# The last stage of a mixture-of-experts layer: one gate matrix per 64 tokens, the residual accumulated in PSUM, normalisation in two vector operations

## The chip, the core and the metric

The kernel runs on one core of a Trainium2 chip. The metric is the device time of one execution in microseconds (us). A core has five engines that run side by side and wait for each other through semaphores: TensorE (PE in the profile), VectorE (DVE), ScalarE (ACT), GpSimd (POOL) and SyncE (SP, which issues most transfers). PE writes its results to PSUM, in banks of 512 float32 numbers per partition; everything else lies in SBUF (128 partitions) or in HBM.

## The reference, cut to what matters

One encoder layer over 1024 tokens of 1024 numbers: a mixer, a layer norm that gives `x1`, and a mixture of experts in which each token takes two experts out of 32. The change touches only how the two experts' rows of a token are brought together and normalised:

```
gate  = pg_sel * softmax(top two expert logits)        # two gates a token
f     = gate[:,0]*expert_row_0 + gate[:,1]*expert_row_1
x     = layer_norm(ALPHA*x1 + g2*f) * ln2_gain + ln2_bias   # the output
layer_norm(z) = (z - mean(z)) * rsqrt(var(z) + 1e-5)   # over the 1024 numbers of a token
```

## The kernel before

Some 950 us go to the mixer, the rest to `experts()`. There the tokens are gathered by expert into blocks of up to 128, 64 or 32 rows; a block goes through gate and up projections (`head`, lines 1689 and 1697), a transposition (`turn`) and the down projection (`down`, lines 1717 and 1728). For blocks of 64 and 32 rows the matrix multiplications use 64 or 32 columns of the array each and write to their own part of the PSUM partitions. The rows, already multiplied by `g2`, are scattered to `ys_d` in HBM by POOL, so that row `2*token + j` holds the j-th expert's row of a token. Three weight buffers of each kind are used in turn, and once the experts are through, their space takes the data of the last stage.

The last stage begins in `finish` (line 1562) on SP: it loads the gain and bias (`late`), `x1` in two transfers (`x1a`, `x1b`, lines 1570 to 1573), waits for the last scattered rows, and loads `ys_d` in eight transfers of 1 MB, one for each tile of 128 tokens (line 1577). Before the change partition p of a tile holds both rows of token p, 8 KB in one piece.

`tail_plan` (line 1800) writes the work of the last stage on PE, ACT and DVE as three lists. Each engine runs its list in the written order and waits, ahead of an entry, for the entries named with it. For each of the eight tiles:

- `dg0`, `dg1`: diagonal 128x128 matrices with a tile's gates, one for each j, made once on ACT and DVE.
- `product` (PE): for each half of 512 numbers, `dg0` times the first rows plus `dg1` times the second, accumulated in a PSUM bank. In tiles 2 and 5 (`inside`) a third multiplication adds `ALPHA*x1`.
- `sums`: in tiles 2 and 5 ACT copies the bank to SBUF and sums it up on the way; in the other six DVE adds `ALPHA*x1` and sums up (`scalar_tensor_tensor`, line 1835).
- `mean` (DVE), `deviation` (ACT: `sq` sums up the squares, `sd` takes the root), `rstd` (DVE: reciprocal and one product), `normal` (ACT: `xn`, scale and shift in one), `affine` (DVE: times gain, plus bias).
- SP writes the tile out (line 1621) once `add` is done.

The products take three pairs of PSUM banks in turn (`pf`, line 1816), so the product of tile t waits for the sums of tile t-3. In float32 PE runs each multiplication of the lists as two instructions; the profile counts those.

Of the kernel before, what the change touches and what calls it, by code (L numbers as in the profile page):

```python
# [123 lines left out]
class Builder:  # L124
# [1336 lines left out]
    def experts(self):  # L1461
# [9 lines left out]

        gain, bias = self.late[:, 0], self.late[:, 1]
# [15 lines left out]
        names += [f"l{i}" for i in range(8)] + ["x1a", "x1b", "tail_pe", "tail_act", "tail_dve"]  # L1488
# [60 lines left out]
        tail = self.tail_plan(sem, yall, x1a, of, ls, gain, bias, [(pgu[0], pgu[1]), tuple(pT), tuple(py)], junk)  # L1549
        with nc.Block() as blk:  # L1550
            @blk.sync
            def _(e):
# [64 lines left out]
                e.dma_start(g2, self.rows_d[3]).then_inc(sem("g2"), 16)  # L1617
                step(0, None)
# [162 lines left out]
            def _(e):  # L1781
# [12 lines left out]

                pipeline(e, lambda g, t: evac_T(e, g, t, 1), head, lambda g, t: [out(e, g, t, q) for q in range(2)], None)
# [4 lines left out]
    def tail_plan(self, sem, yall, x1a, of, ls, gain, bias, banks, junk):  # L1800
# [8 lines left out]
        dg, eps = self.late[:, 2:4].rearrange("p a (j n) -> p (a j) n", n=128), self.leps  # L1809
        gates = self.gtw.rearrange("p j t -> p (j t)")  # L1810
        ident, alpha = self.C["ident"], self.C["alpha"]
# [3 lines left out]
        inside = lambda tt: tt in (2, 5)  # L1815
        pf = lambda tt: banks[tt % 3]

        def product(tt):
            def f(e):
                n = 3 if inside(tt) else 2  # L1820
                for h in range(2):
                    for j in range(n):
                        i = e.matmul(pf(tt)[h], dg[:, tt + 8 * j] if j < 2 else alpha,  # L1823
                                     (yall[tt][:, j] if j < 2 else x1a[tt])[:, hs[h]], start=j == 0, stop=j == n - 1)
                return i
            free = [("sum1", tt - 3)] if tt > 2 else []
            op("pe", "mm", tt, [("dg0", tt), ("dg1", tt), (f"l{tt}", 16), ("x1" + "ab"[tt // 4], 16)] + free, f)

        def sums(tt):
            for h in range(2):  # L1830
                if inside(tt):
                    op("act", f"sum{h}", tt, [("mm", tt)], lambda e, h=h: e.activation(
                        of[tt][:, hs[h]], pf(tt)[h], AF.Copy, accum_out=col(tt, h)))
                else:
                    op("dve", f"sum{h}", tt, [("mm", tt), ("x1" + "ab"[tt // 4], 16)], lambda e, h=h: e.scalar_tensor_tensor(  # L1835
# [3 lines left out]
        def mean(tt):  # L1839
            op("dve", "mean", tt, [("sum1", tt)], lambda e: e.tensor_scalar(  # L1840
                col(tt, 12), col(tt, 0), col(tt, 1), -1.0 / D, op0=OP.add, op1=OP.mult))

        def rstd(tt):
# [3 lines left out]
        def affine(tt):  # L1847
            op("dve", "gain", tt, [("xn", tt), ("late", 32)], lambda e: e.tensor_mul(of[tt], of[tt], gain))  # L1848
            op("dve", "add", tt, [("gain", tt)], lambda e: e.tensor_add(of[tt], of[tt], bias))  # L1849
# [7 lines left out]
        def normal(tt):  # L1857
            op("act", "xn", tt, [("rs", tt)], lambda e: e.activation(of[tt], of[tt], AF.Identity, bias=col(tt, 16),
                                                                    scale=col(tt, 15)))


        for tt in range(8):
            op("act", "dg0", tt, [], lambda e, j=tt: e.activation(dg[:, j], ident, AF.Copy, scale=gates[:, j:j + 1]))
            op("dve", "dg1", tt, [], lambda e, j=tt + 8: e.tensor_scalar(dg[:, j], ident, gates[:, j:j + 1], None,
                                                                        op0=OP.mult))
# [100 lines left out]
```

## Time and profile before

| | |
|---|---|
| time before, median of 3 runs | 1594.07 us (1593.53 to 1601.02) |
| the profiled execution | 1595.89 us, of which span 1594.0 us |
| busy over the span | PE 87%, DVE 49%, ACT 36%, POOL 24% |
| mean granted clock of PE | 0.915 of full speed |
| the last stage | from the first load of `ys_d` at 1541.62 to the end of the span |

A busy share is an average over stages with different limits. The last stage is some 52 us of 1594, and what a change there is worth is read from its own stretch: which engine the chain of waits runs through, when the first tile can begin, and what comes after the last sum. Times with two decimals that stand alone (1547.12) are us from the start of the span.

### The profile page before, as it was taken

The numbers are of one execution on the slowest core, as the hardware profiler recorded it, in microseconds if no ns is written. First come the engines' busy times: TensorE is split into PE (matmuls) and PEld (weight loads), VectorE is DVE, ScalarE is ACT, GpSimd is POOL, SyncE is SP. The second block draws the span as 40 slices with busy tenths as digits, with TensorE's granted clock in tenths as the row PEclk, the third lists the DMA queues.
The fourth block names the chain that finished last, engine by engine and source line by source line (L and its number), as shares of the span: only waits on it lengthen the run. The fifth ranks groups of instructions, "written<-read, shape, count | busy, mean of one in ns | idle before, by whom it ended". The sixth has DMA issues, their size and how long they took to land. (4 is left out here: it accounts for less than half of the span.)

```text
span 1594.0 us, 25797 instructions
## 1 busy us (share of the span) xinstructions
PE 1383.6 (87%) x8638; PEld 1014.9 (64%) x8638; DVE 779.3 (49%) x2015; ACT 573.9 (36%) x1196; POOL 379.0 (24%) x442
## 2 busy tenths in 40 slices
PE   6999999978869899899999728999998898789866
PEld 5778777766656677676788725676764575566522
DVE  6776786845974666655668851111111111111127
ACT  5663332414566777676444320000000010000006
POOL 3331332350347115601323141100110011101000
PEclk8999999987869899989999758999999999899978
DMA  9868999866413217117383648878978877887674
GB/s 256 221 195 309 290 296 332 285 221 179 134 51 105 80 41 204 39 53 219 95 322 121 250 173 353 338 296 305 376 275 310 334 298 279 333 337 307 253 268 201
DMA packets 163401, 371.94 MB, mean 233 GB/s; under 512 B 22880, under 2 KB 99009, under 8 KB 154227
## 3 DMA queue, kind: packets, MB, share of 16 engines
q1 hardware_dynamic: 155555, 350.59, 62.0%
q0 software_dynamic: 7632, 18.51, 3.6%
q8 instruction: 133, 2.18, 0.6%
q14 instruction: 81, 0.66, 0.1%
HBM read 365.47 MB, written 65.44 MB: 270 GB/s over the span
## 5 line engine op out<-in xcount | busy, mean ns | idle before, releaser
L1689 PE MATMUL m_pgu<-w,m_xT 128*128 128x256 f32 x896 | 200.1, 385 | 7.0 <-issue 7.0
L1689 PEld LDWEIGHTS m_pgu<-w,m_xT 128*128 128x128 f32 x896 | 171.5, 193 | 31.9 <-issue 8.2
L1697 PE MATMUL m_pgu<-w,m_xT 128*32 128x256 f32 (+1 forms) x1312 | 119.1, 459 | 38.8 <-issue 38.8
L1638 POOL DMA_INDIRECT ys_s<-m_y,m_idx x37 | 35.0, 946 | 494.4 <-DVE m_y L1756 299.9
L196 PE MATMUL pg<-uh,w_h 128*128 128x512 f32 x320 | 127.1, 404 | 2.2 <-ACT uh L294 1.6
L197 PE MATMUL pg<-ul,w_h 128*128 128x512 f32 x320 | 128.8, 402 | 0.2 <-POOL ul L295 0.2
L198 PE MATMUL pg<-uh,w_l 128*128 128x512 f32 x320 | 127.4, 398 | 0.0
L1697 PEld LDWEIGHTS m_pgu<-w,m_xT 128*32 128x32 f32 (+1 forms) x1312 | 56.6, 127 | 91.4 <-issue 76.4
L1789 DVE TENSOR_TENSOR m_h<-m_sil,m_pgu 128x256 f32<-128x256 f32 x28 | 11.8, 421 | 192.6 <-ACT m_sil L1765 192.6
L1717 PE MATMUL m_py<-w,m_hT 128*128 128x512 f32 x224 | 99.6, 597 | 0.0
L1793 DVE TENSOR_TENSOR m_h<-m_sil,m_pgu 64x256 f32<-64x256 f32 (+1 forms) x23 | 10.8, 471 | 160.2 <-ACT m_sil L1768 156.4
L1765 ACT ACTIVATE m_sil<-m_pgu 128x256 f32<-128x256 f32 x28 | 10.7, 383 | 196.1 <-PE m_pgu L1689 196.1
L210 DVE SCALAR_TENSOR_TENSOR acc<-wm,sc_c,acc 128x256 f32<-128x256 f32 x112 | 62.0, 554 | 31.9 <-DMA wm<-in_w_mod_dram 22.1
L1773 ACT COPY m_hT<-m_ph 128x128 f32<-128x128 f32 (+2 forms) x37 | 14.8, 401 | 165.3 <-PE m_ph L1705 165.3
L1717 PEld LDWEIGHTS m_py<-w,m_hT 128*128 128x128 f32 x224 | 41.4, 190 | 47.3 <-issue 46.9
L196 PEld LDWEIGHTS pg<-uh,w_h 128*128 128x128 f32 x320 | 61.0, 192 | 15.8 <-ACT uh L294 1.8
L197 PEld LDWEIGHTS pg<-ul,w_h 128*128 128x128 f32 x320 | 61.5, 192 | 14.4 <-POOL ul L295 0.9
L198 PEld LDWEIGHTS pg<-uh,w_l 128*128 128x128 f32 x320 | 61.4, 192 | 13.6 <-issue 0.7
L945 DVE SCALAR_TENSOR_TENSOR sn<-s,fc,sf 64x64 f32<-64x64 f32 x168 | 47.6, 283 | 41.8 <-PE s L936 38.7
L756 PE MATMUL g<-zi,bk 64*128 64x128 f32 x384 | 54.2, 319 | 15.2 <-DMA bk<-bkd 9.5
L1768 ACT ACTIVATE m_sil<-m_pgu 64x256 f32<-64x256 f32 (+1 forms) x23 | 9.8, 427 | 153.9 <-PE m_pgu L1697 153.9
L756 PEld LDWEIGHTS g<-zi,bk 64*128 64x128 f32 x384 | 46.5, 217 | 27.8 <-issue 10.3
(521 smaller groups left out, 3090.6 us busy)
## 6 DMA issues: line engine op xcount, KB each, us to landing
w<-in_moe_w_gate_dram SPq DMA_DIRECT2D x37, 2048.0 KB, 8.7
w<-in_moe_w_up_dram SPq DMA_DIRECT2D x37, 2048.0 KB, 12.9
w<-in_moe_w_down_dram SPq DMA_DIRECT2D x37, 2048.0 KB, 15.5
wm<-in_w_mod_dram SPq DMA_DIRECT2D x128, 128.0 KB, 4.5
w<-in_w_in_dram SPq DMA_DIRECT2D x21, 512.0 KB, 6.6
hd<-h SPq DMA_DIRECT2D x18, 512.0 KB, 4.5
wm<-in_w_mod_dram SPq DMA_DIRECT2D x16, 512.0 KB, 6.6
w<-ys_s SPq DMA_DIRECT2D x8, 1024.0 KB, 13.0
```

What stands on the lines that cost most here:

```text
L196: mm(out, lh[0], rh[0], start=start, stop=False)
L197: mm(out, lh[0], rh[1], start=False, stop=False)
L198: mm(out, lh[1], rh[0], start=False, stop=stop)
L210: nc.vector.scalar_tensor_tensor(acc, wm, self.sc_c[:, k:k + 1], acc, op0=OP.mult, op1=OP.add)
L756: nc.tensor.matmul(pa[h][:, j], bk[hs, j], zr[hs, j], start=True, stop=True)
L945: nc.vector.scalar_tensor_tensor(sn[H[h], H[h]], p[H[h], 2, H[h]], fc[H[h]], sf[H[h], H[h]], op0=OP.mult, op1=OP.add)
L1638: e.indirect_dma_start(out=self.ys_d, out_offset=off(idx[0:t, NP + g:NP + g + 1]), in_=y[0:t, g % NY], in_offset=None, bounds_check=2 * S ...
L1689: i = mm(pgu[q][:, o:o + 256], xT[:, k], w[:, k, 256 * q:256 * q + 256], start=k == 0, stop=k == 7)
L1697: i = mm(pgu[0][o:o + t, 0:n], xT[:, k, 0:t], w[:, k, c:c + n], start=k == 0, stop=k == 7)
L1717: i = mm(py[nh], hT[:, 128 * f:128 * f + 128], wd[b][:, f, 512 * nh:512 * nh + 512], start=f == 0, stop=f == 3)
L1773: e.copy(hT[:, 0:n], ph[:, 0:n]).then_inc(sem("hs"), 1)
L1789: e.tensor_mul(h[:, c], sil[:, c], pgu[q][:, 256:512]).then_inc(sem("h"), 1)
```

## The change

1. **One matrix for 64 tokens.** SP loads `ys_d` by another pattern: partition p of tile t now holds rows 256t+p and 256t+128+p, two pieces of 4 KB. Partition p of half s belongs to token 64s + p//2 and to j = p%2, so one 128x64 matrix (a one at column p//2, times the gate of row p) adds both gated rows of 64 tokens in one multiplication. `pair` holds the ones, `rowg` the gates in that order; `rowg` is filled by four small transfers at the start of `experts()`. A product is now four multiplications of 64 columns a tile (two halves of tokens, two of the 512), each to 64 of the PSUM partitions, and each half of 512 has a list entry of its own (`mm0`, `mm1`).
2. **`x1` into PSUM.** In tiles 0 to 6 (`inside`) `residual` multiplies `x1` by `ALPHA` times the identity into the banks first, and the products accumulate on it; ACT does their sums. Only tile 7 is added on DVE. The residuals of tiles 0 and 1 stand at the head of PE's list.
3. **Normalisation.** `centre` (`xm`) takes (z - mean)*gain and `normal` takes that times 1/deviation plus bias, each one `scalar_tensor_tensor` over 128x1024 on DVE. `xn` on ACT, the two vector operations of `affine` and the product `rs` go.

The core of the diff (the new wiring of the names through `experts()` is left out):

```diff
-                        e.dma_start(yall[tt], self.ys_d[256 * tt:256 * tt + 256, :].rearrange("(t j) n -> t j n", j=2)
+                        e.dma_start(yall[tt], self.ys_d[256 * tt:256 * tt + 256, :].rearrange("(s p) n -> p s n", s=2)
...
+                for s in range(2):
+                    for j in range(2):
+                        e.dma_start(rowg[j:128:2, s, :], self.gtw[64 * s:64 * s + 64, j, :]).then_inc(sem("rowg"), 16)
...
+                e.tensor_add(pair, ident[:, 0:128:2], ident[:, 1:128:2]).then_inc(sem("pair"), 1)
...
-        inside = lambda tt: tt in (2, 5)
+        inside = lambda tt: tt < 7
...
+        def residual(tt):
+            def f(e):
+                for h in range(2):
+                    i = e.matmul(pf(tt)[h], alpha, x1a[tt][:, hs[h]], start=True, stop=False)
+                return i
+            op("pe", "x1", tt, [("x1" + "ab"[tt // 4], 16)] + [(f"sum{h}", tt - 3) for h in range(2) if tt > 2], f)
...
+            def half(e, h):
+                for s in range(2):
+                    i = e.matmul(pf(tt)[h][64 * s:64 * s + 64, :], dg[:, 2 * tt + s], yall[tt][:, s, hs[h]],
+                                 start=not inside(tt), stop=True)
...
-            op("dve", "rs", tt, [("rec", tt)], lambda e: e.tensor_mul(col(tt, 16), col(tt, 12), col(tt, 15)))
-            op("dve", "gain", tt, [("xn", tt), ("late", 32)], lambda e: e.tensor_mul(of[tt], of[tt], gain))
-            op("dve", "add", tt, [("gain", tt)], lambda e: e.tensor_add(of[tt], of[tt], bias))
-            op("act", "xn", tt, [("rs", tt)], lambda e: e.activation(of[tt], of[tt], AF.Identity, bias=col(tt, 16),
-                                                                    scale=col(tt, 15)))
+        def centre(tt):
+            op("dve", "xm", tt, [("mean", tt), ("mm1", tt), ("late", 32)], lambda e: e.scalar_tensor_tensor(
+                xm(tt), of[tt], col(tt, 12), gain, op0=OP.add, op1=OP.mult))
+            op("dve", "add", tt, [("rec", tt), ("xm", tt), ("sq", tt)], lambda e: e.scalar_tensor_tensor(
+                of[tt], xm(tt), col(tt, 15), bias, op0=OP.mult, op1=OP.add))
...
+        for tt in range(2):
+            residual(tt)
         for tt in range(8):
+            if tt > 1 and inside(tt):
+                residual(tt)
             product(tt)
-        for tt in range(10):
-            if 0 < tt < 9:
-                rstd(tt - 1)
+        for tt in range(9):
             if tt < 8:
                 if not inside(tt):
                     sums(tt)
                 mean(tt)
-            if tt > 1:
-                affine(tt - 2)
-        for tt in range(9):
-            if tt < 8 and inside(tt):
-                sums(tt)
+                centre(tt)
             if tt:
                 normal(tt - 1)
-            if tt < 8:
-                deviation(tt)
+        for tt in range(8):
+            if inside(tt):
+                sums(tt)
+            deviation(tt)
```

Up to the last stage the order of every engine is the same but for `rowg` on SP and `pair` on DVE. PE's list for the tiles 0 to 2, before; `m_pgu`, `m_pT` and `m_py` are the three pairs of banks, `w_7635` a tile's rows, `m_xg` the gate matrices, `cst` the identity times ALPHA, and a row's last column its output:

```order
-L1823 MATMUL m_pgu<-w_7635,m_xg 128x512 [waits DMAHW6_49,m_x1a,m_tail_dve,m_tail_act]
-L1823 MATMUL m_pgu<-w_7635,m_xg 128x512 x3
-L1823 MATMUL m_pT<-w_7635,m_xg 128x512 [waits DMAHW7_49,m_tail_dve,m_tail_act]
-L1823 MATMUL m_pT<-w_7635,m_xg 128x512 x3
-L1823 MATMUL m_py<-w_7635,m_xg 128x512 [waits PE_49,m_tail_dve,m_tail_act]
-L1823 MATMUL m_py<-w_7635,m_xg 128x512
-L1823 MATMUL m_py<-w,cst 128x512
-L1823 MATMUL m_py<-w_7635,m_xg 128x512 x2
-L1823 MATMUL m_py<-w,cst 128x512
```

The same place now:

```order
+L1828 MATMUL m_pgu<-w,cst 128x512 [waits m_x1a]
+L1828 MATMUL m_pgu<-w,cst 128x512
+L1828 MATMUL m_pT<-w,cst 128x512 x2
+L1835 MATMUL m_pgu<-w_7635,m_xg 64x512 [waits DMAHW6_49,m_tail_dve,m_tail_act]
+L1835 MATMUL m_pgu<-w_7635,m_xg 64x512 x3
+L1835 MATMUL m_pT<-w_7635,m_xg 64x512 [waits DMAHW7_49,m_tail_dve,m_tail_act]
+L1835 MATMUL m_pT<-w_7635,m_xg 64x512 x3
+L1828 MATMUL m_py<-w,cst 128x512 x2
+L1835 MATMUL m_py<-w_7635,m_xg 64x512 [waits PE_49,m_tail_dve,m_tail_act]
+L1835 MATMUL m_py<-w_7635,m_xg 64x512 x3
```

Four multiplications that wait for `x1` alone now stand ahead of the first that waits for `ys_d`, and a tile has two of 128 and four of 64 columns instead of four (tiles 2 and 5: six) of 128.

DVE's list for the last three tiles, before (`m_ls` holds the columns of sums, means and deviations, `w_8648` the tiles themselves):

```order
-L1835 SCALAR_TENSOR_TENSOR w_8648,m_ls<-w,m_pT 128x512 [waits m_tail_pe]
-L1835 SCALAR_TENSOR_TENSOR w_8648,m_ls<-w,m_pT 128x512
-L1840 TENSOR_SCALAR m_ls<-m_ls 128x1 [waits m_tail_dve]
-L1848 TENSOR_TENSOR w_8648<-w_8648,m_xg 128x1024
-L1849 TENSOR_TENSOR w_8648<-w_8648,m_xg 128x1024 [waits m_tail_dve]
-L1844 RECIPROCAL m_ls<-m_ls 128x1 [waits m_tail_act]
-L1845 TENSOR_TENSOR m_ls<-m_ls 128x1 [waits m_tail_dve]
-L1848 TENSOR_TENSOR w_8648<-w_8648,m_xg 128x1024
-L1849 TENSOR_TENSOR w_8648<-w_8648,m_xg 128x1024 [waits m_tail_dve]
-L1848 TENSOR_TENSOR w_8648<-w_8648,m_xg 128x1024 [waits m_tail_act]
-L1849 TENSOR_TENSOR w_8648<-w_8648,m_xg 128x1024 [waits m_tail_dve]
```

The same end now, from the mean of tile 6:

```order
+L1853 TENSOR_SCALAR m_ls<-m_ls 128x1 [waits m_tail_act]
+L1860 SCALAR_TENSOR_TENSOR w_8648<-w_8648,m_ls,m_xg 128x1024 [waits m_tail_pe,m_tail_dve]
+L1864 RECIPROCAL m_ls<-m_ls 128x1
+L1865 SCALAR_TENSOR_TENSOR w_8648<-w_8648,m_ls,m_xg 128x1024 [waits m_tail_dve]
+L1848 SCALAR_TENSOR_TENSOR w_8648,m_ls<-w,m_pT 128x512 [waits m_x1b,m_tail_pe]
+L1848 SCALAR_TENSOR_TENSOR w_8648,m_ls<-w,m_pT 128x512 [waits m_tail_pe]
+L1853 TENSOR_SCALAR m_ls<-m_ls 128x1 [waits m_tail_dve]
+L1860 SCALAR_TENSOR_TENSOR w_8648<-w_8648,m_ls,m_xg 128x1024 [waits m_tail_dve]
+L1864 RECIPROCAL m_ls<-m_ls 128x1 [waits m_tail_act]
+L1865 SCALAR_TENSOR_TENSOR w_8648<-w_8648,m_ls,m_xg 128x1024 [waits m_tail_dve]
+L1864 RECIPROCAL m_ls<-m_ls 128x1 [waits m_tail_act]
+L1865 SCALAR_TENSOR_TENSOR w_8648<-w_8648,m_ls,m_xg 128x1024 [waits m_tail_dve]
```

The mean of tiles 0 to 6 now waits for ACT, the last gain and bias lie one tile behind instead of two, and `sums` stand on DVE only for tile 7.

ACT's list for the tiles 1 and 2 now (a tile is two copies with a sum, the squares, the root):

```order
+L1845 ACTIVATE w_7635,m_ls<-m_pT 128x512 [waits m_tail_pe] x2
+L1869 ACTIVATE w,m_ls<-w_7635,m_ls 128x1024 [waits m_tail_dve]
+L1871 ACTIVATE m_ls<-m_ls,m_le 128x1 [waits m_tail_act]
+L1845 ACTIVATE w_7635,m_ls<-m_py 128x512 [waits m_tail_pe] x2
+L1869 ACTIVATE w,m_ls<-w_7635,m_ls 128x1024 [waits m_tail_dve]
+L1871 ACTIVATE m_ls<-m_ls,m_le 128x1 [waits m_tail_act]
```

Within a tile ACT now waits for DVE's mean between its sums and its squares, and nothing of another tile stands in between.

## Rows read from the trace of the kernel before

**Rows 1.** The page's first line.

```profile
span 1594.0 us, 25797 instructions
```

**Rows 2.** Chain of waits, 1540 to 1594: start, us, engine or transfer, line.

```profile
1541.62 5.25 DMA w<-ys_s
...
1547.12 5.97 PE m_pgu L1823 x8
1553.09 3.43 PE m_pT L1823 x8
...
1573.73 1.27 ACT w L1832 x4
```

**Rows 3.** Timeline, last 4 us: start, duration, engine, line, operation.

```profile
1589.77 1.23 DVE L1849 TENSOR_TENSOR w<-w,m_xg 128x1024 f32<-128x1024 f32 x1
1591.03 0.33 SPq L1621 DMA_DIRECT2D out_dram<-w  x1
```

**Rows 4.** Stretches: us, busy by engine (instructions), granted clock, DMA share, GB/s.

```profile
core 0: us, PE busy (x) PEld busy (x) DVE busy (x) ACT busy (x) POOL busy (x), PEclk, DMA share, GB/s
...
1526.00:1528.00 2.00, 1.32 (x25) 0.58 (x13) 1.28 (x3) 0.00 (x0) 0.00 (x0) 1.00 1.03 414
1535.00:1537.00 2.00, 0.72 (x4) 0.00 (x0) 1.25 (x2) 0.67 (x3) 0.00 (x0) 1.00 0.00 0
1549.00:1551.00 2.00, 2.00 (x4) 0.97 (x3) 0.00 (x0) 0.00 (x0) 0.00 (x0) 0.50 0.98 406
1560.00:1580.00 20.00, 20.00 (x48) 8.74 (x46) 16.11 (x36) 15.95 (x29) 0.00 (x0) 1.00 0.43 173
```

**Rows 5.** Chain of waits in two expert blocks, down projection, 64 and 128 rows.

```profile
1004.37 3.58 PE m_py L1728 x16
...
1499.64 7.06 PE m_py L1717 x16
```

**Rows 6.** Timeline, ACT and DVE in the last stage, 1555 to 1576.

```profile
1555.98 1.28 ACT L1854 ACT_TABLE_LOAD   x1
...
1566.48 0.68 DVE L1835 SCALAR_TENSOR_TENSOR w<-w,m_pgu 128x512 f32<-128x512 f32 x1
...
1567.20 0.21 DVE L1840 TENSOR_SCALAR m_ls<-m_ls 128x1 f32<-128x1 f32 x1
...
1567.45 1.15 ACT L1852 ACTIVATE w<-w,m_ls 128x1024 f32<-128x1024 f32 x1 [0.23 <-DVE m_ls L1840]
...
1568.73 0.29 ACT L1854 ACTIVATE m_ls<-m_ls,m_le 128x1 f32<-128x1 f32 x1
...
1575.03 0.21 DVE L1840 TENSOR_SCALAR m_ls<-m_ls 128x1 f32<-128x1 f32 x1 [0.82 <-ACT w L1832]
```

**Rows 7.** Timeline, DVE and POOL in the mixer, 152 to 157 and 278 to 284.

```profile
154.12 1.28 DVE L655 SCALAR_TENSOR_TENSOR o_k<-z,cw,o_k 128x1024 f32<-128x1024 f32 x1
155.32 0.42 DVE L432 SCALAR_TENSOR_TENSOR row<-pm,bm 128x256 f32<-128x256 f32 x1
...
279.00 1.47 POOL L722 TENSOR_TENSOR kd<-kd,kd 128x512 f32<-128x512 f32 x1
279.24 2.31 DVE L654 SCALAR_TENSOR_TENSOR o_k<-z,cw,o_k 128x1024 f32<-128x1024 f32 x1
```

**Rows 8.** Lines 1571 and 1577: issue (ns, first and last start), time to landing.

```profile
L1571 SPq DMA_DIRECT2D w<-x_s x2: 432/470/508, 1517.3 to 1517.7; - x2
DMA to landing us min/median/max: 10.7/13.2/15.7
...
L1577 SPq DMA_DIRECT2D w<-ys_s x8: 332/456/755, 1541.6 to 1545.3; - x8
DMA to landing us min/median/max: 5.3/13.0/19.7
```

**Rows 9.** Start of `experts()`: SP's first transfer, PE's first expert product.

```profile
L1617 SPq DMA_DIRECT2D m_g<-rows_s x1: 326/326/326, 949.6 to 949.6; - x1
...
956.09 6.18 PE L1697 MATMUL m_pgu<-w,m_xT 128*32 128x256 f32 x64 [0.61 <-issue]
```

**Rows 10.** Timeline, the gate matrices on DVE before the last stage.

```profile
1538.88 1.66 DVE L1864 TENSOR_SCALAR m_xg<-cst,m_gt 128x128 f32<-128x128 f32 x8 [1.75 <-issue]
```

More of the change, by code (lines that the diff above doesn't have):

```diff
@@ L1470, in experts @@
         ls = sb("m_ls", [128, 8, 20])
+        pair = sb("m_pair", [128, 64])
+        rowg = sb("m_rowg", [128, 2, 8])
         gain, bias = self.late[:, 0], self.late[:, 1]
@@ L1487, in experts @@
         names = ["T0", "T1", "xT", "gu0", "gu1", "sil", "h", "ht", "hs", "y0", "y1", "e0", "e1", "late", "g2", "o"]
-        names += [f"l{i}" for i in range(8)] + ["x1a", "x1b", "tail_pe", "tail_act", "tail_dve"]
+        names += [f"l{i}" for i in range(8)] + ["x1a", "x1b", "pair", "rowg", "tail_pe", "tail_act", "tail_dve"]
         names += [f"{w}{b}" for w in "GUD" for b in range(NB)]
@@ L1547, in wait @@
                 e.wait_ge(sem(name), v)
-        tail = self.tail_plan(sem, yall, x1a, of, ls, gain, bias, [(pgu[0], pgu[1]), tuple(pT), tuple(py)], junk)
+        tail = self.tail_plan(sem, yall, x1a, of, ls, gain, bias, pair, rowg, [(pgu[0], pgu[1]), tuple(pT), tuple(py)], junk)
         with nc.Block() as blk:
@@ L1797, in experts, with tail_plan @@
         ctx.close()
-    def tail_plan(self, sem, yall, x1a, of, ls, gain, bias, banks, junk):
+    def tail_plan(self, sem, yall, x1a, of, ls, gain, bias, pair, rowg, banks, junk):
         lists = {"pe": [], "act": [], "dve": []}
@@ L1807, in op @@
             where[name, tt] = eng, len(lists[eng])
-        dg, eps = self.late[:, 2:4].rearrange("p a (j n) -> p (a j) n", n=128), self.leps
-        gates = self.gtw.rearrange("p j t -> p (j t)")
-        ident, alpha = self.C["ident"], self.C["alpha"]
+        dg, eps = self.late[:, 2].rearrange("p (j n) -> p j n", n=64), self.leps
+        alpha = self.C["alpha"]
         hs = [slice(0, 512), slice(512, D)]
         col = lambda tt, i: ls[:, tt, i:i + 1]
-        inside = lambda tt: tt in (2, 5)
+        inside = lambda tt: tt < 7
         pf = lambda tt: banks[tt % 3]
-        def product(tt):
[L1819 to L1824, printed above, removed]
-                return i
-            free = [("sum1", tt - 3)] if tt > 2 else []
-            op("pe", "mm", tt, [("dg0", tt), ("dg1", tt), (f"l{tt}", 16), ("x1" + "ab"[tt // 4], 16)] + free, f)
+        def residual(tt):
[4 more added lines that the diff above has]
+            op("pe", "x1", tt, [("x1" + "ab"[tt // 4], 16)] + [(f"sum{h}", tt - 3) for h in range(2) if tt > 2], f)
+        def product(tt):
+            def half(e, h):
+                for s in range(2):
+                    i = e.matmul(pf(tt)[h][64 * s:64 * s + 64, :], dg[:, 2 * tt + s], yall[tt][:, s, hs[h]],
+                                 start=not inside(tt), stop=True)
+                return i
+            for h in range(2):
+                free = [(f"sum{h}", tt - 3)] if tt > 2 else []
+                op("pe", f"mm{h}", tt, [("dg0", tt), ("dg1", tt), (f"l{tt}", 16)] + free, lambda e, h=h: half(e, h))
         def sums(tt):
@@ L1831, in sums @@
                 if inside(tt):
-                    op("act", f"sum{h}", tt, [("mm", tt)], lambda e, h=h: e.activation(
+                    op("act", f"sum{h}", tt, [(f"mm{h}", tt)], lambda e, h=h: e.activation(
                         of[tt][:, hs[h]], pf(tt)[h], AF.Copy, accum_out=col(tt, h)))
                 else:
-                    op("dve", f"sum{h}", tt, [("mm", tt), ("x1" + "ab"[tt // 4], 16)], lambda e, h=h: e.scalar_tensor_tensor(
+                    op("dve", f"sum{h}", tt, [(f"mm{h}", tt), ("x1" + "ab"[tt // 4], 16)], lambda e, h=h: e.scalar_tensor_tensor(
                         of[tt][:, hs[h]], x1a[tt][:, hs[h]], ALPHA, pf(tt)[h], op0=OP.mult, op1=OP.add,
@@ L1855, in deviation @@
                                                                     scale=1.0 / D))
[L1857 to L1859 removed]
         for tt in range(8):
[L1863 to L1864 removed]
+            after = [("pair", 1), ("rowg", 64)]
+            op("act", "dg0", tt, after, lambda e, tt=tt: e.activation(dg[:, 2 * tt], pair, AF.Copy, scale=rowg[:, 0, tt:tt + 1]))
+            op("dve", "dg1", tt, after, lambda e, tt=tt: e.tensor_scalar(dg[:, 2 * tt + 1], pair, rowg[:, 1, tt:tt + 1], None,
                                                                         op0=OP.mult))
+        for tt in range(2):
+            residual(tt)
         for tt in range(8):
+            if tt > 1 and inside(tt):
+                residual(tt)
             product(tt)
[L1868 to L1870 removed]
+        for tt in range(9):
             if tt < 8:
```

6 lines of the change are left out of this document (3 added, 3 removed).

## The prediction

> **What bounds the kernel now.** I read the page first for the span [rows 1], then the chain of waits from its end, then the timeline of the last stage, and only then looked in earlier stages for operations that the change brings in. The profiled execution took 1595.89 us, 1.89 more than its span; the median of the runs is 1594.07. I work out a difference in the span and take it off the median.
>
> In the chain the reader is to see three links of the last stage [rows 2]. The first load of scattered rows is issued at 1541.62 and its tile can be multiplied at 1547.12. From there PE is the chain: tile 0 takes 5.97 us, tile 1 takes 3.43, and so on to 1573.73. Then come the sums of tile 5 on ACT and, from 1575.03 [rows 6], DVE alone: sums, gain, bias of the tiles that are left. The last bias operation ends at 1589.77 + 1.23 = 1591.00; the write-out of that tile ends the span 3.00 us later [rows 3, 1]. The stretch 1560 to 1580 shows why both matter: PE busy all 20 us, DVE 16.11, ACT 15.95, POOL nothing [rows 4]. So the stage is bound by PE at first and by DVE at the end, and the change cuts both.
>
> PE's clock explains the long tile 0: at 1535 to 1537 it is granted in full (2.4 GHz); after the pause until 1547 the row of 1549 to 1551 shows 0.50 (1.2 GHz), and from 1560 on it is full again [rows 4]. Tile 0 and tile 1 both are eight instructions on PE; the difference 5.97 - 3.43 = 2.54 us is what the half clock costs.
>
> **The change part by part.**
>
> *Products of 64 columns.* A product becomes eight instructions of 64 columns, alternating between two parts of PSUM. An expert block of 64 rows does just that in its down projection: sixteen such instructions in 3.58 us, against 7.06 for sixteen of 128 columns, both at full clock [rows 5]. Two of 64 columns run side by side. A product is then 1.79 us, before 3.43. From below: half of 7.06 is 3.53, so 1.77; from above, without overlap, 3.53.
>
> *Residuals.* Two multiplications of 128 columns, four instructions, half of 3.43: 1.72 us. Those of tiles 0 and 1 wait only for `x1`, which was issued at 1517.3 and 1517.7 and landed within 15.7 us [rows 8], by 1533.4. PE is free from about 1535.7 (0.72 us busy after 1535 [rows 4]). Eight instructions take 3.43 us at full clock, 6.9 at half, so they end by 1542.6 and the wait for the rows hides them. If PE came to them as late as 1540.2 they would still fit. The clock falls again in the pause of 4 us or more that is left, as it did before: I take the same 2.54 us off tiles 0 and 1, although nothing fixes that (a rival below).
>
> *PE's lane.* Tiles 0 and 1 need sixteen instructions: 1547.12 + 3.58 + 2.54 = 1553.24. Five tiles (2 to 6) of 1.72 + 1.79 = 3.51 follow: 1570.79. The second half's sum on ACT is half of the four rows' 1.27, and 0.03 later the mean starts [rows 2, 6]: mean of tile 6 at 1571.47.
>
> *ACT's lane.* It now has seven tiles' sums in a row with the squares. One tile: sums 1.27; 0.03 to the mean; from the mean to the squares 1567.45 - 1567.20 = 0.25; to the root 1568.73 - 1567.45 = 1.28; root 0.30: 3.13 us [rows 2, 6]. No other tile's work lies in the 0.28 us of that round trip. Start: products of tile 0 at half clock, 3.58, end at 1550.7; sum and mean 0.68, then 0.25, 1.28, the table load before the first root 1.28 [rows 6], 0.30: sums of tile 1 at 1554.5. Five tiles on, 1570.15, and 1.30 to the mean of tile 6: 1571.45. ACT and PE come out level, so gaining on one alone would bring nothing.
>
> *DVE's lane.* A `scalar_tensor_tensor` of 128x1024 with a column and a tensor takes 1.28 us, and the next independent one starts 1.20 after it (154.12 to 155.32) [rows 7]. A tile: mean 0.25, `xm` 1.20, reciprocal 0.19, `add` 1.20 = 2.84, less than ACT's 3.13, so DVE waits for ACT and no longer sets the pace. What stands behind its waits is only its own next tile. After the last mean on ACT's pace (tile 6, 1571.47) the end is: 0.25 + 1.20 (`xm` 6) + 0.19 + 1.20 (`add` 5) + 0.61 (first sum of tile 7) + 0.72 (second and its read-out, 1566.48 to 1567.20 [rows 6]) + 0.25 + 1.20 (`xm` 7) + 0.19 + 1.20 (`add` 6) + 0.19 + 1.28 (`add` 7) = 8.48, at 1579.95. The root of tile 7 is ready: its squares start with `xm` 7 and take 1.28 + 0.30, while DVE needs 2.59 up to that reciprocal. PE delivered tile 7 at 1570.79 + 1.79, before DVE asks at 1574.3. Plus the write-out 3.00: span end 1582.95.
>
> *Loads of two 4 KB pieces.* `x1` already comes in 4 KB pieces: 414 GB/s at 1526 to 1528, against 406 for the 8 KB pieces at 1549 to 1551 [rows 4]. Value: nothing. Slack: the last tile lands at 1545.3 + 19.7 = 1565.0 [rows 8] and PE wants it at 1570.8. Only the first tile's 5.25 us is on the path; a tenth more or less of the rate over 1 MB is 0.25 us either way.
>
> *Gate matrices, `rowg`, `pair`.* The matrices are half as wide; before, DVE had its eight done at 1540.5 [rows 10], 6 us ahead of the first product, so saving there brings nothing. The four small transfers stand on SP behind one issued at 949.6 and ahead of the first expert's release. At 0.33 each they cost SP 1.3 us; PE's first expert product starts only at 956.09, waiting for gathered rows [rows 9]. Value 0; from above 1.3 if the gather lands that much later; no gain, since work is only added.
>
> *Sum.* 1582.95 - 1594.0 = -11.05 us. On the profiled execution 1584.8, on the median **1583.0 us**, 0.69% less. About 0.5% (8 us) is what a measurement of this kernel can tell from no change.
>
> *A rule that speaks against it.* After 1004.37 + 3.58 the next piece of the chain, of another width, follows at 1007.95, and the sixteen narrow instructions took 0.05 us more than half of the wide ones [rows 5]: here a change of width costs 0.05 us at most. The Trainium skill ("TensorEngine Tiling (Array Packing)", section Key Properties) says that changing the tiling mode drains the engine; it gives no time for it. By that rule the sum would rise at every change of width, by the rows at hand hardly; what a larger cost would do is the third rival.
>
> **The rivals.**
>
> 1. *The clock is already up at 1547.* For it: the early residuals put work where PE was idle, and if they start late they run right up to the products. Against: by my times a pause of over 4 us remains, and in the pause before the clock did fall. PE would save 2.54, but ACT only the 1.79 by which its first sum comes earlier: 1594.07 - 11.05 - 1.79 = 1581.2.
> 2. *The change of width drains the array.* Price: one lost slot of a wide instruction, 3.43 / 8 = 0.43, at each of the ten changes from tile 1's products to tile 6's: +4.3, 1587.3. Against: the 0.05 above.
> 3. *DVE's two-tensor operations run at 2.31 us instead of 1.28, and the kernel gets slower.* For it: the same form took 2.31 beside a POOL operation [rows 7], and all sixteen of the new ones have two tensors in SBUF. A tile on DVE would be 0.25 + 2.23 + 0.19 + 2.23 = 4.90; from the mean of tile 1 (1555.8) six tiles make 1585.2, then 1.33 for tile 7's sums, 0.25, three operations of 2.23, 2.23 and 2.31 and two reciprocals of 0.19: 1593.9, span end 1596.9, time 1597.0. It decides from 2.1 us an operation on. Against: POOL has nothing to do in the last stage (0.00 in the stretch of 1560 to 1580 [rows 4]). The Trainium skill ("SBUF — State Buffer", section Who interferes with whom) names the cause: such an operation takes its second input through a port shared with GpSimd. By that rule, too, an idle POOL leaves 1.28; the trace agrees.
> 4. *Narrow multiplications with different matrices don't overlap.* In the expert block of rows 5 both parts of the array hold the same matrix, here they hold different ones. A product would be 3.53, PE's tile 5.25: tiles 0 and 1 to 1547.12 + 7.06 + 2.54 = 1556.72, tile 6 at 1583.0, plus 0.68, 8.48 and 3.00: 1595.1, time 1595.2, no change that can be told.
>
> **How the numbers follow.** Forecast 0.66, by itself 1580 to 1586 (clock phase and 0.3 us a tile either way). Rival 1: 0.13. Rival 2: 0.09. Rival 3: 0.04. Rival 4: 0.04. The other 0.04 goes to a start delayed by the small transfers or the first load, 1584 to 1588. The range 1579.8 to 1588.5 leaves out rivals 3 and 4 and the ends of the others. Faster by over 0.5% means below 1586.1: nearly all of the forecast (0.61) and rival 1 (0.13), a third of rival 2 (0.03) and half of the rest (0.02): 0.79. Slower needs over 1602: rival 3 at its worst, 0.02. The rest, 0.19, is within 0.5%.
>
> **What would show it.** PE: eight residual instructions between 1536 and 1543; then tiles of 3.5 us, of which the eight narrow instructions take 1.8. ACT: sums of consecutive tiles about 3.1 to 3.5 us apart. DVE: operations of 1.28 us, idle before each mean, and some 8.5 us from tile 6's mean to the last `add`. The write-out ends 11 us earlier. I am wrong if narrow pairs take 0.43 us an instruction, if a gap stands at each change of width, if the new vector operations take over 2 us, or if the first product starts later than some 5.5 us after the first load is issued.

## The result, and the profile after

| | before | after |
|---|---|---|
| time, median of 8 runs each | 1593.8 us (1589.49 to 1601.02) | 1582.9 us (1574.12 to 1588.67) |
| ratio | | 0.993, 95% interval 0.9902 to 0.9957 |
| profiled execution, its span | 1595.89, 1594.0 us | 1585.84, 1584.0 us |
| the stage: issue of the first load of `ys_d` to the end of the span | 1594.0 - 1541.62 = 52.38 us | 1584.0 - 1541.47 = 42.53 us |

The forecast was 1583.0 us. The stage became 9.85 us shorter, the forecast said 11.05. The loads are issued anywhere from 1533.8 to 1550.1 in the profiles shown here, because what stands before them doesn't take the same time in every execution: in the two profiles of the changed kernel SP's first transfer of `experts()` already starts at 948.85 and at 955.31. The stage's own length varies less: the changed kernel, profiled again, has 42.62 us (e12 below). What does vary in it is tile 0, which runs at a low clock: 3.62 to 3.77 us with narrow products, but 5.37 to 6.34 for the same eight wide instructions (before 5.97, e1 5.48, e3 5.37, e4 6.34). So what an edit does is read here from the stage, each from one profile, in wide kernels no finer than about 1 us; the median with its interval only says whether it can be told in the time at all.

The chain of waits of the kernel after, from the load to the end (start, us, engine or transfer, line; dots stand for further tiles and for small links), against [rows 2, 3]:

```profile
1541.47 5.37 DMA w<-ys_s
...
1546.98 3.68 PE m_pgu L1835 x8
1550.66 1.86 PE m_pT L1835 x8
1552.52 1.91 PE m_py L1828 x4
1554.44 1.87 PE m_py L1835 x8
...
1567.65 1.91 PE m_pgu L1828 x4
1569.57 1.89 PE m_pgu L1835 x8
1571.48 0.70 ACT w L1845 x2
...
1572.27 0.23 DVE m_ls L1853
...
1572.52 1.29 DVE w L1860
...
1579.68 1.28 DVE w L1865
```

PE is the chain up to the last product but one; a tile is a residual (L1828) of 1.91 us and a product (L1835) of 1.87, where a product of 3.43 stood before. From 1572.27 DVE alone is left, in operations of 1.28 us. The same stretch on ACT, from the timeline (start, duration, engine, line, operation, in brackets the idle time before it and what ended it):

```profile
1560.65 0.58 ACT L1845 ACTIVATE w<-m_pgu 128x512 f32<-128x512 f32 x1
...
1563.72 0.58 ACT L1845 ACTIVATE w<-m_pT 128x512 f32<-128x512 f32 x1
...
1566.84 0.60 ACT L1845 ACTIVATE w<-m_py 128x512 f32<-128x512 f32 x1
...
1567.70 0.60 ACT L1845 ACTIVATE w<-m_py 128x512 f32<-128x512 f32 x1 [0.17 <-PE m_py L1835]
...
1570.62 0.60 ACT L1845 ACTIVATE w<-m_pgu 128x512 f32<-128x512 f32 x1 [0.31 <-PE m_pgu L1835]
```

The first sums of tiles 3 and 4 are 3.07 us apart, ACT's own pace; in tile 5 (1567.70) ACT begins to wait for PE, and from its first sum (1566.84) to tile 6's it is 3.78, PE's pace. The new vector operations by form in the stage (count, then busy us, mean ns, idle us before them):

```profile
L1860 DVE SCALAR_TENSOR_TENSOR w<-w,m_ls,m_xg 128x1024 f32<-128x1024 f32 x8 | 10.3, 1285 | 0.3
L1865 DVE SCALAR_TENSOR_TENSOR w<-w,m_ls,m_xg 128x1024 f32<-128x1024 f32 x8 | 10.3, 1285 | 0.3
```

And the stretches (duration, busy by engine, PE's granted clock, DMA share, GB/s), against [rows 4]:

```profile
1545.00:1547.00 2.00, 0.02 (x2) 0.05 (x2) 0.00 (x0) 0.00 (x0) 0.00 (x0) 0.50 1.03 424
1549.00:1551.00 2.00, 2.00 (x6) 0.53 (x4) 0.00 (x0) 0.98 (x3) 0.00 (x0) 0.54 1.02 414
1551.00:1553.00 2.00, 2.00 (x10) 0.61 (x7) 1.47 (x2) 1.63 (x5) 0.00 (x0) 1.00 1.02 408
```

The clock had again fallen to 1.2 GHz (0.50) in the wait and was back at 2.4 GHz (1.00) in the stretch of 1551 to 1553. The loads come at the rate of before: 414 GB/s in the stretch of 1549 to 1551, before 406.

### The profile page after: what moved, and what is told of

Read it like the earlier page. It is cut to its first block, busy times and chain, and to the rows that moved or that the text cites. A ratio compares the mean times of both kernels' runs of the same rounds, so it can differ in the third digit from the quotient of the medians.

```text
span 1584.0 us, 25843 instructions
## 1 busy us (share of the span) xinstructions
PE 1376.8 (87%) x8658; PEld 1005.5 (63%) x8658; DVE 775.1 (49%) x1988; ACT 570.3 (36%) x1208; POOL 377.9 (24%) x442
## 5 line engine op out<-in xcount | busy, mean ns | idle before, releaser
L1734 PE MATMUL m_py<-w,m_hT 128*32 128x256 f32 (+1 forms) x656 | 57.8, 442 | 7.5 <-issue 6.4
```

Source lines behind the costliest of these rows:

```text
L1734: i = mm(py[0][o:o + t, 0:n], hT[:, 64 * j + t * a:64 * j + t * a + t], wd[b][:, f, c:c + n], start=f == 0, stop=f == 3)
```

## The experiments

Theory, "lanes": the three lists run side by side and the slowest engine a tile sets the pace, so a part is worth what it takes from the engine that is slowest with the other parts in place. Rivals: the parts add up, or one part alone brings everything. The eight combinations of the three parts were run; N is the narrow products with their loads and `rowg`, X is `x1` in PSUM for tiles 0 to 6, M is the new normalisation. Stages are of one profile each, medians of 6 to 10 runs; a ratio is to runs of the kernel before that were taken with them (their medians lie between 1593.72 and 1597.21, so ratios of different rows compare less well than they look):

| parts | run | stage, us | slowest lane | median us | ratio, 95% interval |
|---|---|---|---|---|---|
| none | before | 52.38 | PE, then DVE | 1593.8 | |
| M | e1 | 48.76 | PE | 1589.89 | 0.9986 (0.9962 to 1.001) |
| N | e2 | 48.58 | DVE | 1588.86 | 0.9967 (0.9934 to 0.9999) |
| X | e3 | 55.82 | PE | 1598.08 | 1.0011 (0.9982 to 1.0041) |
| X, M | e4 | 53.51 | PE | 1592.05 | 0.9986 (0.9954 to 1.0018) |
| N, X | e5 | 48.12 | ACT | 1589.27 | 0.9957 (0.9921 to 0.9993) |
| N, M | e6 | 43.52 | DVE | 1585.89 | 0.9963 (0.9934 to 0.9993) |
| N, X, M | after | 42.53 | PE, ACT | 1582.9 | 0.993 (0.9902 to 0.9957) |

**e1: the new normalisation alone.** Each edit is shown in part, "..." stands for what is left out. This one is against the kernel before; `normal` now stands in DVE's list:

```diff
-            if tt > 1:
-                affine(tt - 2)
...
+                centre(tt)
             if tt:
                 normal(tt - 1)
```

> The kernel before with the new normalisation alone: the loads, the wide matrices and the sums stay, the product rs, xn on ACT and gain/bias on DVE are replaced by the two new vector operations. Measure: the last stage, from the issue of the first load of ys_d to the end of the span (before 52.4 us, after the whole change 42.5). Theory of lanes (whichever engine's list is slowest sets the end): DVE has as much work a tile as before (sums 1.33 + 0.25 + 1.20 + 0.19 + 1.20 = 4.17 against 4.12), but gain and bias lie one tile behind instead of two, so one tile's work less is left over at the end: 48.9 us, time about 1590.5. Rival, three parts that each save their own work: as DVE saves nothing a tile, nothing: 52.4.

Measured 1592.5 - 1543.74 = 48.76 us: the lanes' value. PE keeps its wide products to the end (the chain has them up to 1575.46), and the work behind them is shorter. Of the 3.62 us gained, 0.49 is tile 0, which took 5.48 instead of 5.97 on an unchanged list of PE.

```profile
1549.34 5.48 PE m_pgu L1823 x8
...
1575.46 1.27 ACT w L1832 x4
```

**e2: narrow products alone**, with the old normalisation and without early residuals. This edit and all that follow are against the kernel after:

```diff
-        inside = lambda tt: tt < 7
+        inside = lambda tt: tt in (2, 5)
...
-        for tt in range(2):
-            residual(tt)
...
-                centre(tt)
+            if tt > 1:
+                affine(tt - 2)
```

> One matrix for 64 tokens alone: narrow products and the new load pattern, x1 added on DVE in six tiles as before (in PSUM, ahead of the products, in tiles 2 and 5), no early residuals, old normalisation in the old order. Theory of lanes: PE is through by 1568 to 1570 instead of 1580.6, but DVE's 4.1 us a tile then sets the pace from 1551 on: 47.9 us, about 4.5 less than before. Rival of parts that add up: PE's chain of 26.6 us loses 1.6 us for each of the six to seven tiles in it, so most of the gain comes from here: about 42 us.

Measured 1594.2 - 1545.62 = 48.58 us. This is near the lanes' 47.9 and far from the rival's 42. PE is no longer in the chain of the middle tiles, DVE is: sums 1.22, gain 1.14 and bias 1.23 a tile.

```profile
1566.45 1.22 DVE w L1848 x4
...
1567.98 1.14 DVE w L1862
1569.15 1.23 DVE w L1863
```

**e3: `x1` in PSUM alone**, on wide products (loads and normalisation are the old ones too):

```diff
+                    i = e.matmul(pf(tt)[h], dg[:, tt + 8 * j], yall[tt][:, j, hs[h]],
+                                 start=j == 0 and not inside(tt), stop=j == 1)
```

> x1 into PSUM alone, in tiles 0 to 6, with the two early residuals; wide matrices, old loads, old normalisation. Theory of lanes: PE needs 5.15 us a tile and ACT has sums, scale and squares (4.1 us a tile), so the kernel gets slower than before: 56 us, time about 1598. Rival of parts that add up: five tiles' sums leave DVE, which ends the chain (1.33 us each), so some us faster than before: 46 to 49 us.

Measured 1599.3 - 1543.48 = 55.82 us: 3.44 longer than before, as the lanes have it, though the interval of its ratio takes in no change. Tile 0 took 5.37 us here; with the 5.97 of before the loss would be 4.04. The chain of this run also gives the price of a residual beside products of the same width:

```profile
1557.73 1.72 PE m_py L1826 x4
1559.45 3.43 PE m_py L1833 x8
```

It is 1.72 us, the forecast's number, and not the 1.91 of the whole change.

**e4: `x1` in PSUM and the new normalisation, wide products.**

```diff
-                for s in range(2):
...
+                for j in range(2):
+                    i = e.matmul(pf(tt)[h], dg[:, tt + 8 * j], yall[tt][:, j, hs[h]],
...
```

> Products stay 128-wide matrices as before; x1 goes into PSUM in tiles 0 to 6 and the normalisation is the new one. Theory of the three lanes (the end is set by the slowest engine a tile): PE needs 1.72 us for the residual and 3.43 us for the wide products of a tile, 5.15 us, as in the run with x1 in PSUM alone, while ACT (3.1 us a tile) and DVE (2.8 us a tile) wait; from the issue of the first load of ys to the end of the span about 53.4 us (before: 52.4), time about 1595 us, no faster than before. Rival, that each part brings a gain of its own and the gains add up: the new normalisation alone shortened this stretch by 3.6 us, so with it the stretch of the run with x1 in PSUM alone (55.8 us) would come out the same 3.6 us shorter at 52.2 us; and if x1 in PSUM gave DVE's addition back it would fall to 46 to 49 us.

Measured 1590.1 - 1536.59 = 53.51 us, the lanes' 53.4; the same PE tile of 1.72 + 3.43 us stands in its chain. DVE's gain on top (46 to 49) falls. Adding up does not: its 52.2 came from runs with a milder tile 0 than this one's.

```profile
1541.95 6.34 PE m_pgu L1833 x8
```

With 5.97 us for tile 0 in all of them, adding up gives 52.38 - 3.13 + 4.04 = 53.29 (e1's gain less its 0.49, e3's loss as above), and this run 53.14. So e4 doesn't tell adding up from the lanes; e5 and the whole change do.

**e5: narrow products and `x1` in PSUM, old normalisation.**

```diff
-                centre(tt)
+            if tt > 1:
+                affine(tt - 2)
```

> Narrow products and x1 in PSUM for tiles 0 to 6, but the normalisation of before (ACT subtracts the mean and scales, DVE multiplies by gain and adds bias in two operations). Lanes: ACT gets the sums (two halves of 0.6 us) on top of the square, the root and the scaling that it had, about 4.1 us a tile and is the slowest; PE needs 3.78 us, DVE about 2.9 us; issue of ys to the end about 47.8 us, time near 1589 us. Rival, that PE's matrices alone set the end in the whole change: 42.5 us as in the whole change.

Measured 1586.7 - 1538.58 = 48.12 us (47.8 by the lanes, 42.5 by the rival). One tile of its chain, all ACT:

```profile
1555.48 1.15 ACT w L1845 x4
1556.64 1.13 ACT w L1866
1557.77 1.14 ACT w L1870 x2
1558.93 0.29 ACT m_ls L1872
1559.22 1.16 ACT w L1845 x4
```

Sums, scaling, squares, root: 3.74 us a tile, where I had expected 4.1. Five tiles at 4.1 would have made the stage 1.8 us longer, so the agreement to 0.3 us is in part luck. Adding up would give 52.38 - 3.80 + 3.44 = 52.02 us, 3.9 more than measured. Once ACT does the sums, `xn` has to leave ACT, and only the new normalisation takes it away.

**e6: narrow products and the new normalisation, `x1` on DVE in six tiles.**

```diff
-        inside = lambda tt: tt < 7
+        inside = lambda tt: tt in (2, 5)
```

> The whole change but for x1: it is added on DVE in tiles 0, 1, 3, 4, 6 and 7, in PSUM only in tiles 2 and 5 as before, and no residual is early. Theory of lanes: DVE needs 4.17 us in six tiles and 2.84 in two, together some 31 us from about 1550, while PE is done early; that ends level with the whole change: 42.7 us (after: 42.5), so x1 in PSUM brought nothing. Rival, the three parts belong together and x1 in PSUM is what relieves DVE: undone, 1.33 us come back for each of five tiles, 48 to 49 us.

Measured 1577.3 - 1533.78 = 43.52 us, 0.8 above the lanes' value and far from the rival's. `x1` in PSUM is worth only 0.99 us in the whole change: it takes 1.23 us from DVE in each of five tiles and puts about as much on ACT, and on PE 1.91 in the three of them whose residual isn't early.

Both rivals of the theory fall on the eight rows together: no part alone gains more than 3.80 us, and the three add up to 3.62 + 3.80 - 3.44 = 3.98, where the whole change gains 9.85.

**e7: the early residuals.** The whole change without the two residuals at the head of PE's list:

```diff
-        for tt in range(2):
-            residual(tt)
...
-            if tt > 1 and inside(tt):
+            if inside(tt):
```

> The whole change, but the residuals of tiles 0 and 1 are multiplied in order behind the loads of ys, not ahead of them while PE waits. Lanes: two residuals of 1.91 us more on PE behind the arrival of ys, 3.7 us later end: issue of ys to the end 46.2 us, time about 1586.5 us. Rival, that the early residuals matter only by raising the granted clock for the first products: the cold part of the first tile is at most 1.8 us, so at most 44.3 us; if neither matters, 42.5 us.

Measured 1588.5 - 1543.81 = 44.69 us, 2.16 more than with them: between the two numbers on record, and the expectation itself was wrong. The residual of tile 0 still stands ahead of tile 0's product in the list and waits for `x1` alone; in the trace it ran at 1539.73 (first line, from PE's timeline). Only that of tile 1 came behind the rows, and the chain shows it:

```profile
1539.73 1.98 PE L1828 MATMUL m_pgu<-w,cst 128*128 128x512 f32 x4 [1.82 <-issue]
...
1549.35 3.77 PE m_pgu L1835 x8
1553.12 1.98 PE m_pT L1828 x4
1555.11 1.87 PE m_pT L1835 x8
```

One residual moved, 1.98 us on PE's path, 2.16 in the stage. The first product took 3.77 us against 3.68, both at 0.50, so the second early residual doesn't keep the clock up: it saves its own time on PE's path.

**e8: residuals in 64 columns**, so that PE never changes width among the tiles:

```diff
-                    i = e.matmul(pf(tt)[h], alpha, x1a[tt][:, hs[h]], start=True, stop=False)
+                    for s in range(2):
+                        c = slice(64 * s, 64 * s + 64)
+                        i = e.matmul(pf(tt)[h][c, :], alpha[:, c], x1a[tt][:, hs[h]], start=True, stop=False)
```

> The whole change, with the residual too made of 64-column matrices (eight multiplications' worth instead of two wide ones a tile: alpha's columns 0 to 63 and 64 to 127 apart), so that PE never goes from a 64-column to a 128-column matrix inside the chain of tiles. If PE's excess over the forecast (3.78 us a tile measured, 3.51 forecast) is the change of width, the residual returns to 1.72 us or less beside narrow products, a tile to about 3.55 us, issue of ys to the end about 41.2 us, time near 1581.5 us. Rival, that the excess is in starting a new accumulation or in the bank and not in the width: the tile stays at 3.78 us and the stretch at 42.5 us; second rival, that two 64-column multiplications of one residual don't overlap: residual 3.4 us, tile 5.2 us, stretch about 51 us.

Measured 1590.0 - 1548.48 = 41.52 us; time 1583.0 us (four runs), ratio 0.9896 (0.9867 to 0.9925): the median is that of the whole change, and the gain shows in the stage alone. PE's timeline (residual, product, residual):

```profile
1559.42 1.90 PE L1830 MATMUL m_py<-w,cst 128*64 128x512 f32 x8
1561.14 1.90 PE L1837 MATMUL m_py<-w,m_xg 128*64 128x512 f32 x8
1562.85 1.90 PE L1830 MATMUL m_pgu<-w,cst 128*64 128x512 f32 x8
```

From start to start 1.72 and 1.71: a tile is 3.43 us, not 3.78. The excess of 0.35 a tile is the change of width: a wide residual beside wide products (e3) and a narrow one beside narrow products don't have it. The weight loads (PEld) show where it arises, first e8, then the whole change:

```profile
1560.71 0.15 PEld L1837 LDWEIGHTS m_py<-w,m_xg 128*64 128x64 f32 x2 [0.28 <-issue]
...
1554.37 0.20 PEld L1835 LDWEIGHTS m_py<-w,m_xg 128*64 128x64 f32 x4 [0.76 <-issue]
1554.37 1.94 PE L1835 MATMUL m_py<-w,m_xg 128*64 128x512 f32 x8
```

In e8 the matrices of the product of 1561.14 are loaded 0.43 us ahead of it; after a change of width the first load begins only with the product, after 0.76 us without one. How the 0.17 us of a change divide between that load and the end of the work before it, no run here shows. Only 1.0 of the 5 x 0.35 = 1.75 us came out at the end, because now ACT sets the pace with its 3.07 us a tile.

**e9: e8 with other tiles on DVE** (the early residual of tile 1 goes with it):

```diff
-        inside = lambda tt: tt < 7
+        inside = lambda tt: tt not in (1, 2)
```

> The whole change with the residual in 64-column matrices (as in the run before), and with another choice of the tiles whose x1 goes into PSUM: tiles 1 and 2 add x1 on DVE, early, where DVE has time, and tile 7 goes through PSUM and ACT, so that DVE has nothing to add behind the last product. Lanes: PE saves one residual (six instead of seven, 1.72 us) in the chain of tiles, and behind the last product stand the two sums on ACT, the mean and one tile's normalisation instead of the eleven steps that held DVE for 8.7 us; issue of ys to the end about 39.1 us, some 3.4 us less than the whole change, time about 1579.5 us, 0.991 of before. Rival, that DVE is loaded just as much wherever its two additions stand, and only one residual less counts: 41.5 less 1.7 = 39.8 us or, if the ACT lane of 3.1 us a tile with the eighth tile's sums sets the end, 41.5 us and more.

Measured 1582.9 - 1542.90 = 40.00 us; 1581.39 us, 0.9932 (0.9906 to 0.9958). Nearer the rival's 39.8 than my 39.1. Its chain runs through DVE up to 1560.33 and then through ACT, five tiles of 3.07:

```profile
1561.92 1.16 ACT w L1847 x4
...
1563.18 0.22 DVE m_ls L1855
...
1563.43 1.25 ACT w L1871 x2
...
1564.70 0.29 ACT m_ls L1873
1564.99 1.16 ACT w L1847 x4
```

ACT does the sums, waits 0.35 for DVE's mean, squares, takes the root, and begins again.

**e10: e9 with PE kept busy in the wait**, by products into a bank that is overwritten later:

```diff
+                        i = e.matmul(pf(1)[h][c, :], alpha[:, c], x1a[0][:, hs[h]], start=True, stop=True)
...
+        for _ in range(5):
+            fill()
```

> As the run e9_mix, with five further wide products of 64-column matrices that write a bank whose content is thrown away, behind the first residual: PE multiplies for about 10 us while it waits for the load of ys, where it stood still and its granted clock fell to 0.50. If the low clock at the start of the stage costs what the rows show (first tile 3.7 us where a warm one takes 1.72, so about 1.6 to 2.0 us), and PE is on the path there, the stretch from the issue of ys to the end is 37.4 us, 1.6 us less than e9_mix, time about 1578 us. Rival, that the ACT lane sets the end in any case: no change from e9_mix. Second rival, that the multiplications outlast the wait (they start late): up to 2 us longer than e9_mix.

Measured 1580.4 - 1540.71 = 39.69 us; 1582.8 us, 0.9929 (0.9901 to 0.9957). The clock stayed at 1.00 as long as PE had work, but the thrown-away products (line 1839) ended only at 1547.86, some 1.7 us after the rows had come (5.4 us after the issue, as in the whole change).

```profile
1544.00:1546.00 2.00, 2.00 (x12) 0.84 (x10) 0.00 (x0) 0.00 (x0) 0.00 (x0) 1.00 1.04 418
...
1547.49 0.37 PE m_pT L1839
```

So the gain on tile 0 was used up but for 0.3 us: the second rival's mechanism; behind tile 0 the chain is that of e9. By their intervals none of e8, e9 and e10 can be told from the whole change in the time.

**e11: ACT rearranged**, four thrown-away products, tiles 1 and 3 on DVE in place of 1 and 2:

```diff
-        inside = lambda tt: tt < 7
+        inside = lambda tt: tt not in (1, 3)
...
+        for _ in range(4):
+            fill()
...
-        for tt in range(8):
-            if inside(tt):
+        op("act", "root", 0, [], lambda e: e.activation(col(0, 14), eps, AF.Sqrt))
+        for tt in range(9):
+            if tt < 8 and inside(tt):
                 sums(tt)
-            deviation(tt)
+            if tt:
+                deviation(tt - 1)
```

> From the run e10_awake, to find what is left in the stage: ACT takes the sums of a tile ahead of the square of the tile before (so that it doesn't stand still for 0.35 us a tile while DVE works out the mean), the table that the square root needs is loaded while ACT waits for ys (1.28 us in the first tile), x1 goes through DVE in tiles 1 and 3 in place of 1 and 2, and four products are thrown away, not five (they outlasted the wait by more than a microsecond). Lanes: PE with a warm clock and six residuals, 1.72 us each like a product, is then the slowest; issue of ys to the end about 36.9 us, 2.8 us less than e10_awake, time about 1577.5 us. Rival, that DVE sets the end (sixteen operations of 1.28 us and two additions are 24 us): no more than 1 us less than e10_awake, 38.7 us and more.

Measured 1578.5 - 1540.60 = 37.90 us, 1.79 less than e10: more than the rival's 1 us, less than my 2.8; 1580.14 us, 0.9906 (0.9875 to 0.9936). Four things were changed at once, and no run divides the 1.79 between them. PE's timeline at the start shows where the last microsecond is; ahead of it stands the stretch in which the thrown-away products had ended:

```profile
1544.00:1546.00 2.00, 0.42 (x1) 0.00 (x0) 0.00 (x0) 0.00 (x0) 0.00 (x0) 1.00 1.02 414
...
1546.16 1.94 PE L1846 MATMUL m_pgu<-w,m_xg 128*64 128x512 f32 x8 [1.75 <-DMA w<-ys_s]
1548.71 1.94 PE L1846 MATMUL m_pT<-w,m_xg 128*64 128x512 f32 x8 [0.61 <-DMA w<-ys_s]
...
1554.57 1.94 PE L1846 MATMUL m_pgu<-w,m_xg 128*64 128x512 f32 x8 [0.49 <-DMA w<-ys_s]
```

At full clock the first tile takes 1.94 us against 3.68 (both from the start of its first instruction to the end of its last), and now PE waits for the second and the fourth tile's rows: the loads are the next bound.

**e12: the changed kernel again**, beside e11.

> The whole change, unaltered, on the same chip as the run before: issue of ys to the end 42.5 us as in its first profile; time 1583 us. If that stretch differs by over 0.3 us between two profiles of one kernel, stretches of the other runs can't be told apart by less.

Measured 1592.7 - 1550.08 = 42.62 us; 1584.73 us, 0.9938 (0.9907 to 0.997). e11's median is 4.6 us below it and its stage 4.72 us shorter; the intervals of the two ratios overlap, so in the time alone the two aren't told apart with certainty. In the stage they are: the two profiles of the changed kernel differ by 0.09 us.

## Why the prediction was right, point by point

| link | forecast | after |
|---|---|---|
| issue of the load to the first product | 5.50 | 5.51 |
| tiles 0 and 1 on PE | 6.12 | 5.54 |
| tiles 2 to 6 on PE | 17.55 | 18.96 |
| last product to tile 6's mean | 0.68 | 0.79 |
| DVE to the end of the last operation | 8.48 | 8.69 |
| write-out | 3.00 | 3.04 |
| stage | 41.33 | 42.53 |

- **The mechanism held.** Each predicted link is in the chain, in the order and on the engine named. Narrow pairs overlap with different matrices too (rival 4 out: 1.87, not 3.53), DVE's operations take 1.285 with POOL idle (rival 3 out), the small transfers cost nothing: PE's first expert product followed SP's first transfer after 955.22 - 948.85 = 6.37 us, before after 6.49 [rows 9]. The four transfers themselves held SP for 2.42 us, where 1.3 was forecast, and that product came no later for it. The 4 KB pieces cost nothing here.
- **The mis-sized term is the change of width.** The prediction put it at "0.05 us at most", half of 7.06 against 3.58 [rows 5]. But both of these pieces follow multiplications of another form (32*128 in the rows below), so each holds a change itself:

```profile
1003.31 1.07 PE L1672 MATMUL m_pT<-cst,m_xg 32*128 32x32 f32 x8
...
1498.58 1.06 PE L1672 MATMUL m_pT<-cst,m_xg 32*128 32x32 f32 x8 [0.32 <-issue]
```

Against tile 1's eight wide instructions of 3.43 [rows 2], which follow their own width, the same rows give 7.06 - 2 x 3.43 = 0.20 and, two overlapping, 3.58 - 3.43 = 0.15 us a change: the price could be read before the run. e3 and e8 have the residual at 1.72 without a change, and e8 the product at 1.72; in the change they are 1.91 and 1.87. So 0.35 us a tile for two changes, 0.17 each, between my 0.05 and the 0.43 of rival 2, which was a real mechanism at 0.4 of its price (the prediction's remark that the third rival prices it means the second). A gap at each change of width also stands on its list of what would prove it wrong: the gaps came, too small to leave its range. The rule that I weighed (the Trainium skill, "TensorEngine Tiling (Array Packing)", section Key Properties), that a change of tiling mode drains the engine, was the better guide in kind: the trace agrees with it that a change costs something. My product alone, 1.79 from the expert block, was 0.07 too dear, so the tile came out at 3.78 for 3.51, 1.41 us over five tiles.
- **The cold start was milder than assumed**: 5.54 us for tiles 0 and 1, 0.58 less. It varies from run to run: 3.68 + 2.00 = 5.68 in e12. The forecast took over 2.54 from tile 0 of one profile of the kernel before, and the same eight wide instructions take anywhere from 5.37 to 6.34 us in the four wide kernels; nothing fixed that number, as the prediction says itself. e11 shows by doing it that the half clock costs the first tile 1.74 us (1.94 against 3.68); rival 1's mechanism is sound, it just didn't occur by itself.
- **"ACT and PE come out level"** was close: ACT 3.07 a tile (3.13 forecast), and PE, 0.27 dearer a tile, was about 1.1 us later at tile 6's mean: from its first sum of tile 1 at 1554.50, ACT at 3.07 a tile and 1.35 to the mean would have let it begin at 1571.20, and it began at 1572.27. That is why e8 wins 1.0 us and no more.
- **The agreement of 1582.9 with 1583.0 is closer than the working deserves.** The errors partly cancel (+1.41, -0.58, and +0.11, +0.21, +0.04 in the small links), and the stage's +1.20 is less than the medians of one kernel differ: e12 gave 1584.73. The 0.1 us is luck; the stage, 1.2 us off in 11, is the fair measure of the working.

## What to carry to other kernels

Price a three-part change by engines, not by parts: here one part alone gained 3.6 us, another 3.8, the third lost 3.4, and together they gained 9.85, because `x1` in PSUM puts work on PE and ACT, which the narrow products and the new normalisation relieve. In a stage of parallel in-order lists, write down each engine's time a tile and the start and end that don't repeat; that gave the stage of all seven combinations to within 1.2 us, of six of them once the whole change had been measured. Keep one matrix width within a loop of short multiplications (0.35 us a tile on PE, 1.0 us in the stage here), and look for the engine that stands still ahead of the stage: its clock can be kept up there if the filling ends before the data come.

## What the hardware showed that was not expected

- A change between 64- and 128-column float32 multiplications cost 0.17 us on PE (0.35 a tile of two changes, e8 against the change).
- Narrow multiplications by two different slices of the identity overlap as well as those of an expert block: 1.72 us for eight in e8, half of the 3.43 for eight of 128.
- Work on PE only early in a wait doesn't hold the clock: after the residuals, which ended at 1540.1, the stretch of 1545 to 1547 was at 0.50. With work up to the load, as in e10, every stretch up to PE's last product was at 1.00, and so it was in e11, where that work ended 1.75 us ahead of the first product. In e3 the residuals ended at 1544.9, 4.07 us ahead of it; there the stretch of 1547 to 1549 was still at 1.00 and that of 1549 to 1551, with tile 0 under way, at 0.64.
- With two 4 KB pieces a row pair, the last of SP's eight issues of the loads took 2.66 us (before 0.76 at most for any [rows 8]); this is line 1580 of the kernel after, with minimum, median and maximum in ns:

```profile
L1580 SPq DMA_DIRECT2D w<-ys_s x8: 360/495/2661, 1541.5 to 1546.2; - x8
...
DMA to landing us min/median/max: 5.4/13.3/19.7
```

It follows the pattern of the loads: the longest issue is 2.65 to 2.67 us in all ten kernels' profiles with two pieces, and 0.65 to 0.76 in the four with one (before, e1, e3, e4). The last issue began 0.9 us later than before, the landing times of [rows 8] hardly moved, and nobody waited: no run here tells why one issue takes so long.
